# Three weight sums made by adding transfers in HBM, and twelve block pairs in seven products

## The chip, the cores and the metric

The kernel runs on one core of a Trainium2 chip. The metric is device microseconds of that core, the median of three runs. Profiles are of one execution each; times in them count from the start of the execution's span. Engines are named as the profile names them: PE multiplies matrices, DVE and ACT work elementwise, POOL does little here but issue transfers, SP issues nearly all of them.

## The reference

The computation is one decoder layer on 256 tokens plus 16 learned meta tokens, width 2048, all in float32: an RMS norm, one input projection, eight heads of differential attention and four heads of retention side by side, an output projection with a residual add, then a gated MLP and a final RMS norm. Only the MLP matters here:

```python
def conv_glu(u, w_gate, w_up, conv_w, w_down):
    L = u.shape[1]
    g = u @ w_gate
    gp = jnp.pad(g, ((0, 0), (CONV_W - 1, 0), (0, 0)))
    gc = gp[:, 0:L] * conv_w[0]
    for i in range(1, CONV_W):
        gc = gc + gp[:, i:i + L] * conv_w[i]
    return (jax.nn.silu(gc) * (u @ w_up)) @ w_down
...
    u = rmsnorm(h, ffn_norm[l]) * vmask
    h = h + conv_glu(u, w_gate[l], w_up[l], conv_w[l], w_down[l])
```

The hidden width is 5632, 44 blocks of 128. Each weight is used once, so every weight is loaded once.

## The kernel before, in words

Float32 products are made from two halves: a value is rounded to a shorter type (`hi`, by a cast on ACT, L188) and the remainder is kept beside it (`lo`, by a subtraction on DVE, L189). A product is then three matmuls, hi x hi, hi x lo and lo x hi. This is done for the activations and, chunk by chunk as they arrive, for all weights. `load(c)` (L152) issues the load of a chunk of 1 MB on SP's queue, `prep(hf)` splits one half of it (an *entry*), and `ahead(hf)` runs both a few entries before PE needs them: in the down stage loads six entries ahead, splits three.

The stages follow each other: input projection with attention and retention woven in, output projection, then gate and up, then down. **Gate and up** (the loop over `f`, L751) makes one hidden block of 128 per turn: 16 x 3 matmuls for gate, 16 x 2 wider ones for up, then on DVE and ACT the scaling (`g`, L757), the convolution (`c`), the SiLU (`s`), the product `u` and its split into `fhi[:, f]` and `flo[:, f]`. The tiles `g`, `c`, `s` and `ul` (in which `u` stands) have two buffers each.

**Down** multiplies the hidden blocks (256 tokens = two halves m of 128) by `w_down`, four column groups of 512 (n = 2g + j). It runs in two passes g = 0, 1, with two column groups j each. A *plain* entry holds two hidden blocks of one column group, and takes 4 products of 128 x 128 by 128 x 512. The first 20 hidden blocks are handled in 10 *pairs* (`NS = 10`): two hidden blocks, two token halves and two column groups make a 2 x 2 by 2 x 2 block product, which is computed with seven products instead of eight, from sums of activation blocks (*forms*) and sums of weight blocks. The seven products of each pair go to bank (0,0), (0,1), (1,0) and to four extra banks 1, 5, 6, 7, which are joined into the four results at the end of a pass (`joined`, L894).

The forms are made in gate and up when both blocks of a pair are there (L778 to L791): four sums of 128 x 128 on DVE, split into hi and lo, and stored by a POOL transfer to HBM (`sd`). In the down stage SP loads them back (`sf`, L163) ahead of the pair's weights. The weight chunk of a pair (*mixed* chunk) has four blocks of 512 columns, b11, b12, b22, b21. DVE makes four sums from it (L196, L197, L201, L204), each 512 wide, and seven 512-wide operands are split. This is done in four parts, b, d, u, t, each an entry of its own. `down_order()` writes the order of entries out by hand: a few plain entries first, the parts of the pairs with the other plain entries spread evenly between them, a few plain entries last (`LEAD`). Six plain entries of the last column group are held back for the end, where token half 1 is computed in column halves.

SP's queue is in order: a load that waits for its buffer holds the ones behind it. Raw chunks rotate over five buffers in the down stage (three `raw`, `sraw`, and the former `act1`), and `sf` alternates between two (`act2`, `act3`), the room of the activations of earlier stages.

## Time and profile before

| what | value |
|---|---|
| median of three runs | 1166.14 us (1164.39 to 1166.94) |
| profiled execution, its own time | 1161.82 us |
| its span | 1159.9 us |
| PE, DVE, ACT, POOL busy in the span | 1144.7, 919.0, 597.9, 9.7 us |
| moved by the transfers | 240.16 MB, 207 GB/s on average |
| share of SP's queue, of POOL's | 57.7%, 1.3% |

The page gives the busy time of each engine, then 40 slices of 29 us each as digits of tenths, then transfer queues, then the chain of work that ended last, then groups of instructions by line with the names of what they write and read. A group's mean is the duration of one instruction; since neighbours overlap in an engine's pipeline, the distance between starts is shorter. About four per cent of the matmul records are missing in a trace, so their counts are a little low.

### The profile page before, as it was taken

How to read it: one execution, taken by the hardware profiler on the slowest of the kernel's cores; microseconds unless marked ns; L12 is line 12 of the kernel's file. 1: busy time of each engine (PE TensorE's matmuls, PEld its weight loads, DVE VectorE, ACT ScalarE, POOL GpSimd, SP SyncE). 2: the span in 40 equal slices, each digit the busy share in tenths (PEclk: the TensorE clock that was granted, in tenths of full speed). 3: DMA queues.
4: the chain of work that ended last, by engine and by line, in shares of the span. 5: the costliest groups of instructions: out<-in, count | busy, mean ns of one | idle time of the engine just before them, and what ended most of it. 6: DMA issues, size and time to landing. Idle time of an engine off the chain costs nothing.

```text
span 1159.9 us, 20454 instructions
## 1 busy us (share of the span) xinstructions
PE 1144.7 (99%) x7979; PEld 1068.1 (92%) x7979; DVE 919.0 (79%) x1735; ACT 597.9 (52%) x994; POOL 9.7 (1%) x34
## 2 busy tenths in 40 slices
PE   9999999999999999999999999999999999999997
PEld 8999999999999999999999999999999988887876
DVE  7888887667677769777778777777777799999995
ACT  7566665443345445444445444444444455655663
POOL 0000000000000000000000000000000000000000
PEclk9999999999999999999999999999999999999998
DMA  8644546565648777656655555555555477757671
GB/s 308 199 165 159 169 151 185 172 191 165 189 169 246 239 227 262 218 200 220 208 214 210 220 182 183 186 197 194 185 182 181 180 274 273 302 193 285 234 291 72
DMA packets 80991, 240.16 MB, mean 207 GB/s; under 512 B 41858, under 2 KB 49450, under 8 KB 56064
## 3 DMA queue, kind: packets, MB, share of 16 engines
q1 hardware_dynamic: 79024, 232.44, 57.7%
q0 software_dynamic: 1728, 6.29, 1.3%
q8 instruction: 62, 1.02, 0.3%
q14 instruction: 33, 0.27, 0.1%
q10 hardware_dynamic: 144, 0.14, 0.0%
HBM read 227.05 MB, written 11.80 MB: 206 GB/s over the span
## 4 chain that ended last, share of the span: by engine, by line
PE 88%; DVE 5%; DMA 5%; ACT 1%; issue 1%; SPq 0%; DVEq 0%; ACTq 0%
PE mm L443 14%; PE mm L432 10%; PE mm L430 10%; PE mm L431 10%; PE mm L445 7%; PE mm L423 7%; PE mm L422 7%; PE mm L424 7%; PE o L819 4%; PE o L818 4%; PE o L820 4%; DVE wlo L189 1%; DMA rvt<-rhv 1%; DMA raw<-in_w_first_dram 1%; PE x L818 1%; PE x L819 1%
## 5 line engine op out<-in xcount | busy, mean ns | idle before, releaser
L188 ACT CAST whi<-raw 128x1024 fp32r<-128x1024 f32 (+1 forms) x391 | 396.0, 1018 | 385.6 <-PE mm L423 87.0
L189 DVE TENSOR_TENSOR wlo<-raw,whi 128x1024 fp32r<-128x1024 f32 (+1 forms) x391 | 461.5, 1182 | 156.4 <-ACT whi L188 150.5
L443 PE MATMUL mm<-g,whi 128*128 128x512 f32 x704 | 249.1, 392 | 0.0
L422 PE MATMUL mm<-x,whi 128*128 128x272 f32 (+1 forms) x688 | 198.9, 289 | 0.0
L430 PE MATMUL mm<-g,whi 128*128 128x260 f32 x704 | 198.7, 282 | 0.0
L423 PE MATMUL mm<-x,whi 128*128 128x272 f32 (+1 forms) x688 | 198.4, 288 | 0.0
L424 PE MATMUL mm<-x,wlo 128*128 128x272 f32 (+1 forms) x688 | 197.2, 287 | 1.2 <-DVE wlo L189 1.2
L432 PE MATMUL mm<-g,wlo 128*128 128x258 f32 x704 | 198.1, 281 | 0.0
L431 PE MATMUL mm<-g,whi 128*128 128x256 f32 x704 | 194.9, 277 | 0.0
L445 PE MATMUL mm<-g,wlo 128*128 128x256 f32 x660 | 185.1, 281 | 0.0
L443 PEld LDWEIGHTS mm<-g,whi 128*128 128x128 f32 x704 | 132.2, 188 | 25.9
L431 PEld LDWEIGHTS mm<-g,whi 128*128 128x128 f32 x704 | 133.5, 190 | 1.9
L430 PEld LDWEIGHTS mm<-g,whi 128*128 128x128 f32 x704 | 132.2, 188 | 0.0
L432 PEld LDWEIGHTS mm<-g,wlo 128*128 128x128 f32 x704 | 132.0, 187 | 0.0
L424 PEld LDWEIGHTS mm<-x,wlo 128*128 128x128 f32 x688 | 129.6, 188 | 1.4 <-DVE wlo L189 1.4
L422 PEld LDWEIGHTS mm<-x,whi 128*128 128x128 f32 x688 | 129.7, 188 | 0.0
L423 PEld LDWEIGHTS mm<-x,whi 128*128 128x128 f32 x688 | 129.7, 188 | 0.0
L445 PEld LDWEIGHTS mm<-g,wlo 128*128 128x128 f32 x660 | 124.3, 188 | 0.0
L430 PE MATMUL mm<-ys,whi 128*128 128x260 f32 x256 | 71.9, 282 | 0.0
L432 PE MATMUL mm<-ys,wlo 128*128 128x258 f32 x256 | 71.8, 281 | 0.0
L431 PE MATMUL mm<-ys,whi 128*128 128x256 f32 x256 | 70.7, 276 | 0.0
L819 PE MATMUL o<-wlo,fhi 128*128 128x512 f32 x160 | 62.5, 390 | 0.1
(299 smaller groups left out, 1692.7 us busy)
## 6 DMA issues: line engine op xcount, KB each, us to landing
raw<-in_w_in_dram SPq DMA_DIRECT2D x44, 1024.0 KB
raw<-in_w_gate_dram SPq DMA_DIRECT2D x44, 1024.0 KB
raw<-in_w_up_dram SPq DMA_DIRECT2D x44, 1024.0 KB
raw<-in_w_down_dram SPq DMA_DIRECT2D x24, 1024.0 KB
raw<-in_w_mix_dram SPq DMA_DIRECT2D x20, 1024.0 KB
raw<-in_w_out_dram SPq DMA_DIRECT2D x16, 1024.0 KB
sf<-sd SPq DMA_DIRECT2D x20, 512.0 KB
sd<-sh POOLq DMA_DIRECT2D x10, 512.0 KB, 2.9
```

Source lines behind the costliest of these rows:

```text
L188: S.copy(out=hi[:, b:e], in_=src)
L189: V.tensor_tensor(out=lo[:, b:e], in0=src, in1=hi[:, b:e].bitcast(F32), op=ALU.subtract)
L422: PE.matmul(ps[:, :n], wh, xh, start=(k == 0), stop=False)
L423: PE.matmul(ps[:, :n], wh, xl, start=False, stop=False)
L424: PE.matmul(ps[:, :n], wl, xh, start=False, stop=(k == KT - 1))
L430: PE.matmul(ps[:, :NQ + 2], wh, src.cols(k, GO - 2, GL), start=(k == 0), stop=False)
L431: PE.matmul(ps[:, 4:NQ + 2], wh, src.cols(k, GL, GW), start=False, stop=False)
L432: PE.matmul(ps[:, 2:NQ + 2], wl, src.hi(k), start=False, stop=(k == KT - 1))
L443: PE.matmul(ps, wh, src.cols(k, GO + 2, GW), start=(k == 0), stop=(k == KT - 1))
L445: PE.matmul(ps[:, :SEQ], wl, src.cols(k, GO + 2, GL), start=False, stop=False)
L818: PE.matmul(o, ah, wh, start=start, stop=False)
L819: PE.matmul(o, ah, wl, start=False, stop=False)
```

## The change

`NS` goes from 10 to 12: 24 hidden blocks are handled in pairs, and 20 instead of 24 stay plain. The signs of the seven products are arranged differently, so that three of the four weight sums are pure additions of weight blocks. The host's layout puts the blocks in the order w0, w1, w2, w3 (`w_mix`).

The three sums are made in HBM, before the down stage. `sums(g, p0)` takes a batch of two pairs of one pass and lists five POOL transfers, each of which waits for the one before, through their common tile:

1. t23 (two copies) = w3, 1 MB
2. t23 += w0 in both copies, an adding transfer of 1 MB
3. t23[0] += w2, adding, 512 KB
4. t4 = t23[0], 512 KB
5. t4 += w1, adding, 512 KB

Twelve batches make 60 jobs. `paced(t)` puts one job on POOL's queue behind a one-column copy of `t` on POOL; it is called with `g` for each of the 44 blocks and with `u` for every third, 59 times. What is left is issued after the loop.

In the down stage a mixed chunk is loaded by five SP transfers: blocks w0 and w1 (512 KB), the forms (384 KB), t2 and t3 (512 KB), t4 (256 KB), and w2 (256 KB). t4 and w2 go to a tile of their own, `sw`. DVE makes one sum, w2 - w0. The parts are now d, u, c, t: three of 1024 columns and one of 512.

The form S1 (now a difference of two blocks) is stored in `fhi` and `flo` in the place of the block of the pair that no product uses, so three forms instead of four go through HBM. `fhi` and `flo` of that block are filled in their first half only. `act2` and `act3` are each cut in two rooms for `sf` and `sw`. Two joins subtract instead of add.

```diff
-NS = 10
+NS = 12
-PARTS = ("b", "d", "u", "t")
+PARTS = ("d", "u", "c", "t")
+BATCH = 2
+ROOMS = (0, 1, "2a", "2b", "3a", "3b")
...
         if c in mixed:
             g, p = divmod(mixed[c], NS)
-            sf = big.tile([P, 2, 4, P], F32R, tag=f"act{2 + p % 2}", name=f"sf{g}_{p}")
-            keep(nc.sync.dma_start(out=sf.rearrange("p a b c -> p (a b c)").bitcast(F32),
-                                   in_=pools["sd"][p]))
+            sf = big.tile([P, 6 * P], F32R, tag=f"act{2 + p % 2}a", name=f"sf{g}_{p}")
+            sw = big.tile([P, 2 * NW], F32, tag=f"act{2 + p % 2}b", name=f"sw{g}_{p}")
+            td, td4 = pools["td"][g, p]
+            keep(nc.sync.dma_start(out=t[:, :2 * NW], in_=a["w_mix"][g, p][:, :2 * NW]))
+            keep(nc.sync.dma_start(out=sf.bitcast(F32), in_=pools["sd"][p]))
+            keep(nc.sync.dma_start(out=t[:, 2 * NW:], in_=td))
+            keep(nc.sync.dma_start(out=sw[:, :NW], in_=td4))
+            keep(nc.sync.dma_start(out=sw[:, NW:], in_=a["w_mix"][g, p][:, 2 * NW:3 * NW]))
...
-            b11, b12, b22, b21 = [raw[c][:, i * NW:(i + 1) * NW] for i in range(4)]
-            if s == "b":
-                t1 = pools["dn"].tile([P, NW], F32, tag="t1", name=f"t1_{c}")
-                V.tensor_tensor(out=t1, in0=b12, in1=b11, op=ALU.subtract)
-                V.tensor_tensor(out=b12, in0=b22, in1=b12, op=ALU.subtract)
-                raw[c, 1] = t1
-                halves(b11, 0, NW)
-            elif s == "d":
-                V.tensor_tensor(out=b11, in0=b12, in1=b11, op=ALU.add)
-                halves(raw[c][:, 2 * NW:], 0, 2 * NW)
-            elif s == "u":
-                V.tensor_tensor(out=b21, in0=b21, in1=b11, op=ALU.subtract)
-                halves(raw[c][:, :2 * NW], 0, 2 * NW)
+            g, p = divmod(mixed[c], NS)
+            if s == "d":
+                halves(raw[c][:, :2 * NW], 0, 2 * NW)
+            elif s == "u":
+                halves(raw[c][:, 2 * NW:], 0, 2 * NW)
+                V.tensor_tensor(out=raw[c][:, :NW], in0=raw[c][:, 2 * NW:3 * NW],
+                                in1=raw[c][:, :NW], op=ALU.subtract)
+            elif s == "c":
+                halves(pools["sw"][g, p], 0, 2 * NW)
             else:
-                halves(b21, 0, NW)
-                halves(raw.pop((c, 1)), NW, 2 * NW)
+                halves(raw[c][:, :NW], 0, NW)
...
+        def sums(g, p0):
+            n = BATCH
+            t23 = dp.tile([n, P, 2, NW], F32, name=f"t23_{g}_{p0}")
+            t4 = dp.tile([n, P, NW], F32, name=f"t4_{g}_{p0}")
+            t23r = t23.rearrange("n p a c -> (n p) a c")
+            t4r = t4.rearrange("n p c -> (n p) c")
+            w = a["w_mix"][g, p0:p0 + n].rearrange("n p c -> (n p) c")
+            both = lambda i: w[:, i * NW:(i + 1) * NW].unsqueeze(1).to_broadcast([n * P, 2, NW])
+            go = lambda **kw: jobs.append(lambda: keep(nc.gpsimd.dma_start(**kw)))
+            go(out=t23r, in_=both(3))
+            go(out=t23r, in_=both(0), accum_op=ALU.add)
+            go(out=t23r[:, 0], in_=w[:, 2 * NW:3 * NW], accum_op=ALU.add)
+            go(out=t4r, in_=t23r[:, 0])
+            go(out=t4r, in_=w[:, NW:2 * NW], accum_op=ALU.add)
+            for i in range(n):
+                td[g, p0 + i] = (t23[i].rearrange("p a c -> p (a c)"), t4[i])
+
+        def paced(t):
+            if jobs:
+                j = sp.tile([P, 1], F32, tag="pace", name=f"pace{len(jobs)}")
+                keep(nc.gpsimd.tensor_copy(out=j, in_=t[:, 0:1]))
+                jobs.pop(0)()
...
             V.tensor_tensor(out=g, in0=ps[:, :NQ], in1=rstd2, op=ALU.mult)
+            paced(g)
...
-            S.copy(out=fhi[:, f], in_=u)
-            V.tensor_tensor(out=flo[:, f], in0=u, in1=fhi[:, f].bitcast(F32),
+            n = P if f < KP and f % 2 == 0 else SEQ
+            S.copy(out=fhi[:, f, :n], in_=u[:, :n])
+            V.tensor_tensor(out=flo[:, f, :n], in0=u[:, :n], in1=fhi[:, f, :n].bitcast(F32),
                             op=ALU.subtract)
+            if f % 3 == 0:
+                paced(u)
...
+                s1 = fhi[:, f - 1, P:]
+                S.copy(out=s1, in_=sm[:, 0])
+                V.tensor_tensor(out=flo[:, f - 1, P:], in0=sm[:, 0], in1=s1.bitcast(F32),
+                                op=ALU.subtract)
+                sh = fw.tile([P, 2, 3, P], F32R, tag="sh", bufs=1, name=f"sh{p}")
+                S.copy(out=sh[:, 0], in_=sm[:, 1:])
+                V.tensor_tensor(out=sh[:, 1], in0=sm[:, 1:], in1=sh[:, 0].bitcast(F32),
                                 op=ALU.subtract)
...
-                elif y == "b":
-                    product(1, acts(0, 2 * x), wt, 0)
                 elif y == "d":
                     product((0, 0), acts(0, 2 * x + 1), wt, NW)
-                    product((0, 1), forms(x, 3), wt, 0)
+                    product((0, 1), forms(x, 2), wt, 0)
                 elif y == "u":
-                    product(6, forms(x, 1), wt, 0)
-                    product(7, forms(x, 2), wt, NW)
+                    product(6, forms(x, 0), wt, 0)
+                    product(7, forms(x, 1), wt, NW)
+                elif y == "c":
+                    product((1, 0), acts(1, 2 * x + 1), wt, 0)
+                    product(1, acts(0, 2 * x), wt, NW)
                 else:
-                    product((1, 0), acts(1, 2 * x + 1), wt, 0)
-                    product(5, forms(x, 0), wt, NW)
+                    product(5, acts(1, 2 * x), wt, 0)
```

More of the change, by code (lines that the diff above doesn't have):

```diff
@@ L50, with spread, __init__ @@
 LEAD = [(4, 3), (0, HOLD + 3)]
-PARTS = ("b", "d", "u", "t")
+PARTS = ("d", "u", "c", "t")
+BATCH = 2
+ROOMS = (0, 1, "2a", "2b", "3a", "3b")
 RSEQ = [("y", 0), ("g", 0), ("y", 1), ("g", 1), ("y", 2), ("y", 3), ("g", 2), ("g", 3)]
+def spread(tiles):
+    return [(t, i) for t in tiles for i in range(t.shape[1])]
 class Halves:
-    def __init__(self, tiles, off, width, lead=()):
-        self.tiles, self.off, self.width, self.lead = tiles, off, width, lead
-        self.per = KT // len(tiles)
+    def __init__(self, tiles, off, width):
+        self.at, self.off, self.width = spread(tiles), off, width
     def __getitem__(self, ix):
-        k = ix[1]
+        t, i = self.at[ix[1]]
         c = ix[2] if len(ix) > 2 else slice(0, self.width)
-        return self.tiles[k // self.per][(ix[0],) + self.lead + (
-            k % self.per, slice(c.start + self.off, c.stop + self.off))]
+        return t[ix[0], i, c.start + self.off:c.stop + self.off]
 class Packed:
     def __init__(self, tiles):
-        self.tiles = tiles
-        self.per = KT // len(tiles)
+        self.at = spread(tiles)
     def cols(self, k, b, e):
-        return self.tiles[k // self.per][:, k % self.per, b:e]
+        t, i = self.at[k]
+        return t[:, i, b:e]
     def hi(self, k):
@@ L175, in prep @@
         if held < 2:
-            wx = big.tile([P, 2 * 1024], F32R, tag=f"act{2 + held}", name=f"end{held}")
+            hi, lo = [big.tile([P, 1024], F32R, tag=f"act{2 + held}{i}", name=f"end{held}{i}")
+                      for i in "ab"]
         elif c >= nw and (hf - 2 * nw) % 4 == 3:
             wx = big.tile([P, 2 * 1024], F32R, tag="act0", name=f"wx{hf}")
-        else:
-            wx = None
-        if wx is not None:
             hi, lo = wx[:, :1024], wx[:, 1024:]
@@ L706, in trunk_kernel @@
         pump(len(side))
-        gs = Packed([big.tile([P, KT // 4, GW], F32R, tag=f"act{i}", name=f"g{i}")
-                     for i in range(4)])
+        gs = Packed([big.tile([P, KT * n // 8, GW], F32R, tag=f"act{i}", name=f"g{i}")
+                     for i, n in zip(ROOMS, (2, 2, 1, 1, 1, 1))])
         hd = dp.tile([SEQ, D], F32, name="hd")
@@ L795, in trunk_kernel @@
         pools["dn"] = dn
-        pools["sf"], pools["sd"] = {}, sd
+        while jobs:
+            jobs.pop(0)()
+        pools["sf"], pools["sw"], pools["sd"], pools["td"] = {}, {}, sd, td
         fns = {}
@@ L869, in add, with take_off @@
             V.tensor_tensor(out=h, in0=x, in1=h, op=ALU.add)
+        def take_off(h, x):
+            V.tensor_tensor(out=h, in0=h, in1=x, op=ALU.subtract)
         e = 2 * idx
@@ L902, in f2 @@
                     add(t, bank[6])
-                    add(res[0, 1], t)
+                    take_off(res[0, 1], t)
                 def f3():
```

35 lines of the change are left out of this document (20 added, 15 removed).

## The prediction

> **What bounds the kernel now.** I read the page's slices first, then the windows table over the gate and up stage and over stretches of the down stage, then the chain that ended last, then groups and DMA issues.
>
> ```profile
> span 1159.9 us, 20454 instructions
> PE   9999999999999999999999999999999999999997
> DVE  7888887667677769777778777777777799999995
> DMA  8644546565648777656655555555555477757671
> ```
>
> PE is at nine tenths or more in every slice but the last, so only fewer matmuls or fewer stalls can help. In the last seven slices, the down stage, DVE rises to nine tenths and DMA becomes uneven. The profiled execution took 1161.82 us, 1.9 around its span; the median of the three runs, 1166.14, is 4.3 above it. I sum against the span and carry both offsets.
>
> ```profile
> 446.00:920.00 474.00, 474.00 (x3373) 445.29 (x3372) 361.89 (x608) 224.65 (x350) 5.61 (x10) 1.00 0.55 196
> 930.00:940.00 10.00, 10.00 (x45) 8.29 (x45) 9.03 (x13) 6.07 (x8) 0.00 (x0) 1.00 0.97 374
> 1010.00:1020.00 10.00, 10.00 (x46) 8.29 (x45) 9.75 (x13) 6.16 (x9) 0.00 (x0) 1.00 1.00 406
> 1030.00:1040.00 10.00, 10.00 (x46) 8.29 (x45) 10.00 (x15) 6.54 (x13) 0.00 (x0) 1.00 0.05 19
> 1106.00:1108.00 2.00, 2.00 (x11) 1.63 (x10) 1.97 (x3) 0.00 (x0) 0.00 (x0) 1.00 0.90 291
> 1110.00:1120.00 10.00, 9.73 (x43) 7.53 (x41) 9.48 (x13) 6.11 (x9) 0.00 (x0) 1.00 0.99 409
> ```
>
> The columns are PE, PEld, DVE, ACT and POOL busy (instructions), PE clock, DMA share, GB/s. In gate and up PE is busy all 474 us, DVE 362 (76%), POOL 6, and the DMA engines stand at 0.55. In the down stage DVE is close to or at 10 of 10 us; DMA runs at 406 GB/s in one stretch and 19 in another.
>
> ```profile
> L818 PE MATMUL o<-whi,fhi x160: 388/389/504, 920.7 to 1143.5; 128*128 128x512 f32 x160
> ...
> 930.06 0.39 PE L820 MATMUL o<-wx,flo 128*128 128x512 f32 x1
> ...
> 932.33 0.39 PE L818 MATMUL o<-whi,fhi 128*128 128x512 f32 x1
> ...
> 1150.13 0.28 PE L818 MATMUL oe<-end,fhi 128*128 128x256 f32 x1
> ...
> 1151.45 0.28 PE L820 MATMUL oe<-end,flo 128*128 128x256 f32 x1
> ```
>
> Pace: the second and third rows are ten steps of 512-column matmuls in 2.27 us, 0.227 each; the last two are eleven steps of 256 columns in 1.32, 0.12 each. The down stage has 20 pairs' chunks of 7 products and 24 plain chunks of 8, 332 products of three matmuls. Twelve products (the held block of six entries) run as column halves. So 960 x 0.227 + 72 x 0.12 = 226.2 us (0.2267 unrounded), while the stage lasts from 920.7 to 1151.4, 230.7. PE stalls there for only about 4.5 us in all.
>
> ```profile
> 1015.51 0.24 PE o L820
> 1015.82 1.06 ACT whi L188
> ...
> 1024.01 0.60 DVE raw L197
> 1024.61 1.14 DVE wlo L189
> ...
> 1046.95 1.14 ACT whi L188 x2
> 1048.14 0.50 PE o L818
> ...
> 1104.76 7.81 DMA raw<-in_w_mix_dram
> ```
>
> Where those go: from 1015.8 the chain leaves PE and stays on DVE through the sums of L196 to L204, the splits of L189 and the joins, until 1048. The last step shown is a mixed chunk's load that took 7.8 us from SP's issue, just ahead of its use. The chain also gives DVE's back-to-back prices: 0.60 us for a 512-wide operation, 1.14 for a 1024-wide one.
>
> **The change, part by part.**
>
> Products. Two more pairs per group become seven products instead of eight: 4 products over both groups, 12 x 0.2267 = **-2.7 us** of PE. This is on the path, as PE has almost no idle.
>
> DVE sums in the down stage.
>
> ```profile
> L204 DVE TENSOR_TENSOR raw<-raw 128x512 f32<-128x512 f32 x20 | 13.8, 689 | 0.2
> L196 DVE TENSOR_TENSOR t<-raw 128x512 f32<-128x512 f32 x20 | 13.8, 688 | 2.2 <-DMA raw<-in_w_mix_dram 2.1
> ```
>
> These are two of the four sums per mixed chunk, 80 in all. A mixed chunk now costs DVE seven 512-wide operations (four sums, three splits) and two 1024-wide splits: 7 x 0.60 + 2 x 1.14 = 6.5 us. After, one sum, one 512-wide split and three 1024-wide: 4.6. Plain entries cost 1.14. Between two mixed chunks the order puts 17/10 plain entries in group 0 and 15/10 in group 1 before, 13/12 and 11/12 after. PE needs 4.76 us for seven products and 2.72 for a plain entry. So, per mixed chunk with its plain entries, DVE against PE: 8.4 of 9.4 and 8.2 of 8.8 us before, joins and final scaling on top; 5.9 of 7.7 and 5.7 of 7.3 after. In total DVE sheds (20 x 6.48 + 48 x 1.14) - (24 x 4.62 + 40 x 1.14) = 28 us, all off the path except what the 4.5 us of stalls owe to it. Bounds of that term: 0 to -4.5. I take **-3**: the DVE-led stretch before 1048 and the small stalls of group 1 go, some turn-over at the change of groups (take(0,1) and take(1,1) must free banks) stays.
>
> ```profile
> L188 ACT CAST whi<-raw 128x1024 fp32r<-128x1024 f32 x63 | 65.6, 1051 | 39.6 <-DVE raw L201 17.6 <-PE o L820 15.4 <-PE x L820 2.7
> L188 ACT CAST whi<-raw 128x512 fp32r<-128x512 f32 x30 | 18.6, 621 | 19.0 <-DMA raw<-in_w_mix_dram 11.6 <-DVE raw L204 5.8 <-DVE wlo L189 1.2
> ```
>
> ACT's casts go from 20 x (2 x 1.05 + 3 x 0.62) + 48 x 1.05 = 130 to 24 x (3 x 1.05 + 0.62) + 40 x 1.05 = 132 us, a little over half the stage: no term.
>
> Loads in the down stage.
>
> ```profile
> raw<-in_w_down_dram SPq DMA_DIRECT2D x24, 1024.0 KB
> raw<-in_w_mix_dram SPq DMA_DIRECT2D x20, 1024.0 KB
> sf<-sd SPq DMA_DIRECT2D x20, 512.0 KB
> sd<-sh POOLq DMA_DIRECT2D x10, 512.0 KB, 2.9
> ```
>
> Per mixed chunk SP moved 1024 + 512 KB; now 512 + 384 (sf without S1) + 512 + 256 + 256 = 1920 KB, in five issues. With its plain entries that is 2.53 MB per 7.7 us in group 0, 2.45 per 7.25 in group 1: 329 and 337 GB/s, against 263 and 267 before. The window row of 1010 to 1020 shows 406 at share 1.00, so the new demand is 83% of what the engines have done here. I take **0**; cover is the remaining 17% and the five raw buffers.
>
> ```profile
> L164 SPq DMA_DIRECT2D sf<-sd x20: 326/327/424, 919.5 to 1104.3; - x20
> ...
> SPq L164 <- PE x L820: 150.7, 18, 17.6
> ```
>
> SP stood 151 us at the sf load, which could not start until the pair two earlier had used its last form, in the fourth part. After, the forms are used in the first two parts, so sf comes free some 3 us earlier, and half of the raw chunk goes ahead of that wait. Queued behind it are td, t4, the third block and the next plain chunk; td is wanted first, one period and about 1 us after the release, less three entries of preparation (about 4.4 us), and sf and td together take about 2.3 us at 406 GB/s. SP issues three more transfers a chunk at 0.33 us each, inside its waits. The first lands behind four lead entries (10.9 us) as before.
>
> Gate and up: the new work. DVE and ACT make forms for twelve pairs, not ten, with one 128-wide copy and subtract more per pair and one half-width split less; PE, busy for all of the 474 us, covers it, with 24% of DVE free. Without that cover it would be the two pairs' own few microseconds. POOL gets 60 transfers, 59 of them paced by a one-column copy of g (44) or u (15), and each later one of a batch waits on POOL for the one before.
>
> ```profile
> L757 DVE TENSOR_TENSOR fg<-mm,rstd x44: 418/426/429, 446.4 to 917.7; 128x258 f32<-128x258 f32 x44
> ...
> 600.10 0.33 SPq L167 DMA_DIRECT2D raw<-in_w_gate_dram  x1
> ...
> 611.33 0.33 SPq L167 DMA_DIRECT2D raw<-in_w_gate_dram  x1
> ...
> 611.81 1.05 ACT L188 CAST whi<-raw 128x1024 fp32r<-128x1024 f32 x1 [1.46 <-issue]
> ```
>
> g is written from 446.4 to 917.7, one per 11.24 us (issue to issue of the same weight), so five jobs of a batch of two pairs have 471/59 x 5 = 39.9 us. Queued behind POOL's wait are the next copy, the next sd store and, through the two g buffers and the two of u, DVE two blocks later. So POOL may be late by about two blocks, 22.5 us, before DVE, ACT and then PE notice; over 12 batches that makes (471 + 22.5)/12 = 41.1 us a batch.
>
> Price of a batch: no row has an adding transfer or one from HBM to HBM. Nearest is the POOL store, 2.9 us for 512 KB. A batch writes 1.5 MB plainly and 2 MB adding, three and four such units. Low end, adding costs nothing extra: 7 x 2.9 = 20 us. High end, an adding unit costs three passes (read, read, write): 3 x 2.9 + 4 x 8.7 = 43.5. I take two passes, 31.9: the stored 512 KB too were read and written within their 2.9, so reading the destination adds one such pass. That is below 41.1: **0** on the path. The high end costs 12 x (43.5 - 41.1) = +29.
>
> Their effect on weight loads: SP issues one per 5.6 us, and the first cast of the 600.10 load comes at 611.81, so a load of 1 MB may take 11.7 us. Shares: 196 GB/s at 0.55 means 356 at full; a batch at two passes is 5.8 MB, 16 us of all engines in 41, or 0.39, together 0.94. It fits, not by much. The page lists both queues as shares of the same 16 engines:
>
> ```profile
> q1 hardware_dynamic: 79024, 232.44, 57.7%
> q0 software_dynamic: 1728, 6.29, 1.3%
> ```
>
> The Trainium skill, page "DMA: Bandwidth & Descriptors", section "Issuing engines are not separate DMA queues", speaks against treating POOL's queue as its own road: transfers from every issuer run on the same 16 engines and interleave. By it a batch would take 16/0.45 = 36 us instead of my 31.9, an estimate that still ends at 0 but brings the point where the queue falls behind (rival A) down from 2.8 passes to 2.4: 41.1 x 0.45 x 356 GB/s is 6.6 MB, less 1.6 plain, over 2.1 MB. The trace agrees as far as these two rows go.
>
> Sum: 1159.9 - 2.7 - 3 = 1154.2 of span; + 1.9 = 1156.1 for a profiled execution; + 4.3 = **1160.4** for the median.
>
> **Rivals.**
>
> A, slower: POOL's chain of adding transfers is dearer than its slots. Place: POOL, then the g and u buffers, in gate and up. It decides from (41.1 - 8.7)/4 = 8.1 us per adding 512 KB, 2.8 passes; each further us costs 48. At three passes: 1160.4 + 29 = 1189. For it: the engines' 0.94, and the chained waits. Against: 31.9 is 9 below.
>
> B, slower: the loads become the bound of the down stage. Windows like 1106 to 1108 gave 291 GB/s at 0.90. At that rate a period takes 8.7 instead of 7.7 and 8.4 instead of 7.25 us, 12 x (1.0 + 1.16) = 26 us on a floor of 226.2 - 2.7 = 223.5. So 249.5 against 230.7, +18.8: 1185. It decides below 337 GB/s. Against: the 406 and 409, and stretches of 0.05 that leave room.
>
> C, no change: only the products count. The stalls were a change of groups and a late load, not DVE's load, and a microsecond of new waiting for td or for bank (0,1), now wanted by the first part of a pair rather than the second, is added: 1166.1 - 2.7 + 1 = 1164.4.
>
> That the sums don't leave the down stage can't be: POOL's order is the program's, and the last batch is wanted 100 us after gate and up end.
>
> **How the numbers follow.** Forecast 0.55, A 0.20, B 0.10, C 0.15. What a measurement here can tell from no change is about 0.2%, 2.3 us. The forecast lies 5.7 below (its own range 1157 to 1163.5: stalls -4.5 to 0 and 1 us of run scatter); it counts as faster, C as the same, A and B as slower: 0.55, 0.15, 0.30. The range goes from 1157 to 1190, past B and the first half of A; what A may cost beyond three passes is left out.
>
> **What would show it.** Products: 328 of them in the down stage, gate and up still one block per 11.24 us with no PE idle. Sums: L196 to L201 gone and DVE near 8 tenths in the down stage. Down stage: 225 us from first o to last oe. A: POOL copies late after their g, fg writes waiting for POOL, block spacing above 11.24. B: casts that wait for raw, sf or sw with DMA share at 1.0. C: 228 us in the down stage. I am wrong if gate and up get longer at all, or if the down stage stays above 228.

## The result and the profile after

| | before | after |
|---|---|---|
| median | 1165.27 us (1162.58 to 1166.94, 4 runs) | 1215.02 us (1213.61 to 1219.32, 4 runs) |
| ratio | | **1.0435** (1.0402 to 1.0469) |
| profiled execution, span | 1161.82, 1159.9 us | 1219.32, 1217.4 us |

The change made the kernel 50 us slower; the prediction was 1160.4 with a range of 1157 to 1190. The profiled execution of the kernel after is the slowest of its four, so the two profiles lie 57.5 us apart. The page of the changed kernel, its slices, its POOL queue and its chain:

```profile
span 1217.4 us, 20806 instructions
PE   9999999999999999989898999999988959999997
DMA  8554455555567779989998989999988898888881
q0 software_dynamic: 19104, 49.81, 20.2%
PE 50%; DMA 25%; issue 18%; POOL 3%; DVE 3%; ACT 1%; SPq 0%; POOLq 0%; DVEq 0%; ACTq 0%
```

PE has slices of 8 at the 18th, 20th, 22nd, 30th and 31st, which lie in gate and up, and one of 5 at the 33rd, in the down stage. DMA stands at eight and nine tenths from the 16th on, where it mostly stood at five to seven. The chain, 88% PE before, goes through DMA for a quarter of the span. Where the time is, by the tiles `fg` and `fhi` (duration minimum, median, maximum; first and last start) and the last matmul:

```profile
L791 DVE TENSOR_TENSOR fg<-mm,rstd x44: 416/427/429, 447.8 to 955.5; 128x258 f32<-128x258 f32 x44
L862 PE MATMUL o<-whi,fhi x158: 388/394/792, 958.5 to 1201.2; 128*128 128x512 f32 x158
1209.10 0.28 PE L864 MATMUL oe<-end0a,flo 128*128 128x256 f32 x1
```

| stretch | before | after | difference |
|---|---|---|---|
| start to the first g | 446.4 | 447.8 | +1.4 |
| first to last g (gate and up) | 471.3 | 507.7 | +36.4 |
| last g to the first o | 3.0 | 3.0 | 0 |
| first o to the last oe (down) | 230.7 | 250.6 | +19.9 |
| the rest | 8.5 | 8.3 | -0.2 |

So of the 57.5 us nearly two thirds lie in gate and up, where the prediction had 0, and a third in the down stage, where it had a gain of 5.7.

**Gate and up.** Who waits for what from 440 to 960 us (us in total, times, longest), in the changed kernel:

```profile
POOL t L767 <- DMA t<-in_w_mix_dram: 312.2, 28, 15.9
...
ACT sh L829 <- DMA sd<-sh: 45.6, 9, 9.4
...
ACT ful L804 <- POOL pace L783: 21.3, 3, 8.9
```

POOL stands 312 us for transfers out of `w_mix`, plain and adding ones, so its queue is late, and two things stand behind it. One is the pacing copy, which holds a buffer of `g` or `ul`: the last of the three rows. The other is the store `sd`, which reads `sh`, a tile with one buffer: ACT cannot write the next forms until the store has landed. POOL's own sequence around one batch (start, duration, and idle before it):

```profile
721.82 1.22 POOL L767 DMA_DIRECT2D t<-in_w_mix_dram  x1
...
738.47 1.36 POOL L767 DMA_DIRECT2D t<-in_w_mix_dram  x1 [14.31 <-DMA t<-in_w_mix_dram]
739.13 1.28 POOL L832 DMA_DIRECT2D sd<-sh  x1
...
753.18 0.92 POOL L767 DMA_DIRECT2D t<-in_w_mix_dram  x1 [12.54 <-DVE mm L440]
...
763.31 0.59 POOL L767 DMA_DIRECT2D t<-t  x1 [8.83 <-DMA t<-in_w_mix_dram]
...
768.57 0.88 POOL L767 DMA_DIRECT2D t<-in_w_mix_dram  x1 [4.37 <-DVE ful L806]
...
770.07 0.89 POOL L767 DMA_DIRECT2D t<-in_w_mix_dram  x1
```

From one issue to the next: the 1 MB copy 16.7 us, the adding 1 MB 14.7, the adding 512 KB 10.1, the copy of 512 KB 5.3, and the last adding one 1.5, since the next batch has another tile and need not wait. (At 753.18 and 768.57 the profile names DVE as the releaser, which is its inference; each of these jobs also waits for the transfer before it, through their tile.) Over all twelve batches the 60 issues go from 449.6 to 991.2, **45.1 us a batch**; the prediction had 31.9, and 41.1 to spend. The issues and what they took to land (medians; the 1 MB row holds the plain copies and the adding ones, twelve each, and the 512 KB row adding ones alone):

```profile
t<-in_w_mix_dram POOLq DMA_DIRECT2D x24, 1024.0 KB, 14.9
t<-in_w_mix_dram POOLq DMA_DIRECT2D x24, 512.0 KB, 8.5
t<-t POOLq DMA_DIRECT2D x12, 512.0 KB, 5.3
sd<-sh POOLq DMA_DIRECT2D x12, 384.0 KB, 13.8
```

The last row is the one to see: the store of the forms, 2.9 us for 512 KB before, takes 13.8 for 384 KB (2.6 for the same 384 KB in f2 below, which issues no sums). It is issued right behind an adding transfer (738.47 and 739.13 above) and lands about when that one does.

**Down.** The head of the stage has a hole. Its timeline:

```profile
974.34 0.40 PE L864 MATMUL x<-whi,flo 128*128 128x512 f32 x1
974.54 0.90 POOL L767 DMA_DIRECT2D t<-in_w_mix_dram  x1 [8.30 <-DMA t<-in_w_mix_dram]
975.11 0.53 POOL L783 COPY pace<-fg 128x1 f32<-128x1 f32 x1
975.66 0.33 SPq L179 DMA_DIRECT2D raw<-in_w_down_dram  x1
...
987.18 1.22 PE L862 MATMUL o<-whi,fhi 128*128 128x512 f32 x2 [12.45 <-ACT whi L198]
```

What SP's queue waited for between 955 and 1030 us:

```profile
SPq L179 <- POOL pace L783: 12.7, 1, 12.7
```

POOL's last copy of a `g` ran at 975.11. The pool `dn`, in which the raw buffer `sraw` lies, takes the room of `fw`, in which `g` lies; so SP could issue this load only then, and PE stood until 987.18. A second hole of 3.3 us ends at 1006. And steps are longer, here ten of 512 columns in 2.33 us where it was 2.27:

```profile
1025.49 0.39 PE L863 MATMUL o<-wx,fhi 128*128 128x512 f32 x1
...
1027.82 0.39 PE L862 MATMUL o<-whi,fhi 128*128 128x512 f32 x1
```

The 328 products have 948 such steps, and 0.006 us each is 5.7 us. PE is idle for 16.3 us of the stage. Against f2 below, which has this stage without sums in 226.2 us, the 250.6 are 24.4 more: 15 of holes (16.3 against 1.2), 5.7 of longer steps, and 3.6 that the profile does not place, part of them behind the holes, where PE's clock is below full (last section).

### The profile page after: what moved, and what is told of

It reads as the page before. It is cut to its first block, busy times and chain, and to the rows that moved or that the text cites. A ratio compares the mean times of both kernels' runs of the same rounds, so it can differ in the third digit from the quotient of the medians.

```text
span 1217.4 us, 20806 instructions
## 1 busy us (share of the span) xinstructions
PE 1164.3 (96%) x7967; PEld 1078.6 (89%) x7967; DVE 891.0 (73%) x1689; ACT 603.5 (50%) x996; POOL 88.5 (7%) x155
## 3 DMA queue, kind: packets, MB, share of 16 engines
q8 instruction: 62, 1.02, 0.3%
## 4 chain that ended last, share of the span: by engine, by line
PE 50%; DMA 25%; issue 18%; POOL 3%; DVE 3%; ACT 1%; SPq 0%; POOLq 0%; DVEq 0%; ACTq 0%
DMA t<-in_w_mix_dram 14%; PE mm L428 6%; PE mm L429 6%; PE mm L427 6%; PE mm L435 4%; PE mm L437 4%; PE mm L436 4%; PE o L863 3%; PE o L864 3%; PE o L862 3%; DMA sd<-sh 2%; PE mm L448 2%; POOL t L767 2%; PE x L863 1%; PE x L864 1%
## 5 line engine op out<-in xcount | busy, mean ns | idle before, releaser
L199 DVE TENSOR_TENSOR wlo<-raw,whi 128x1024 fp32r<-128x1024 f32 x380 | 455.3, 1200 | 171.7 <-ACT whi L198 168.4
L198 ACT CAST whi<-raw 128x1024 fp32r<-128x1024 f32 x380 | 391.6, 1032 | 367.9 <-PE mm L436 85.5
L448 PE MATMUL mm<-g,whi 128*128 128x512 f32 x352 | 128.1, 401 | 5.2 <-ACT whi L198 5.2
L429 PE MATMUL mm<-x,wlo 128*128 128x272 f32 (+1 forms) x344 | 98.6, 287 | 1.2 <-DVE wlo L199 1.2
L427 PE MATMUL mm<-x,whi 128*128 128x272 f32 (+1 forms) x344 | 99.7, 290 | 0.0
L437 PE MATMUL mm<-g,wlo 128*128 128x258 f32 x352 | 99.4, 282 | 0.0
L435 PE MATMUL mm<-g,whi 128*128 128x260 f32 x352 | 99.2, 282 | 0.0
L428 PE MATMUL mm<-x,whi 128*128 128x272 f32 (+1 forms) x344 | 99.2, 288 | 0.0
L448 PEld LDWEIGHTS mm<-g,whi 128*128 128x128 f32 x352 | 68.0, 193 | 19.2 <-ACT whi L198 5.6
L450 PEld LDWEIGHTS mm<-g,wlo 128*128 128x128 f32 x352 | 68.1, 193 | 2.0 <-DVE wlo L199 2.0
L436 PEld LDWEIGHTS mm<-g,whi 128*128 128x128 f32 x352 | 66.6, 189 | 1.9
L435 PEld LDWEIGHTS mm<-g,whi 128*128 128x128 f32 x352 | 66.1, 188 | 0.0
L437 PEld LDWEIGHTS mm<-g,wlo 128*128 128x128 f32 x352 | 66.0, 188 | 0.0
L427 PEld LDWEIGHTS mm<-x,whi 128*128 128x128 f32 x344 | 64.9, 189 | 0.0
```

Source lines behind the costliest of these rows:

```text
L198: S.copy(out=hi[:, b:e], in_=src)
L199: V.tensor_tensor(out=lo[:, b:e], in0=src, in1=hi[:, b:e].bitcast(F32), op=ALU.subtract)
L427: PE.matmul(ps[:, :n], wh, xh, start=(k == 0), stop=False)
L428: PE.matmul(ps[:, :n], wh, xl, start=False, stop=False)
L429: PE.matmul(ps[:, :n], wl, xh, start=False, stop=(k == KT - 1))
L435: PE.matmul(ps[:, :NQ + 2], wh, src.cols(k, GO - 2, GL), start=(k == 0), stop=False)
```

## The experiments

All ratios are to the kernel before, run on the same chip in between; where there is none, the kernel ran once.

| kernel | us | ratio (interval) |
|---|---|---|
| e1_pad | 1212.75 | 1.0396 (1.0368 to 1.0424) |
| e2_sd_on_sp | 1225.25 | one run |
| e3_own_mark | 1211.11 | one run |
| e4_both | 1182.72 | 1.0174 (1.0136 to 1.0212) |
| f1_shift (of before) | 1167.10 | 1.0038 (1.0025 to 1.0052) |
| f2_no_sums | 1158.11 | 0.9964 (0.9951 to 0.9978) |
| f3_early | 1174.43 | 1.0109 (1.0095 to 1.0123) |
| f4_plain | 1163.36 | one run |
| g1_chain | 1195.59 | 1.0286 (1.0263 to 1.0310) |
| g2_two_sums | 1163.24 | 1.0005 (0.9995 to 1.0015) |
| g3_dve_sums | 1175.62 | 1.0107 (1.0088 to 1.0126) |
| g4_norm_on_pool | 1216.43 | one run |
| h1_norm_first | 1212.08 | 1.0418 (1.0393 to 1.0443) |
| h2_chain_norm | 1194.32 | 1.0275 (1.0242 to 1.0308) |
| i1_scale_late | 1179.09 | 1.0133 (1.0111 to 1.0155) |
| i2_chain_late | 1166.11 | 1.0026 (1.0012 to 1.0041) |
| **j1_mixed** | **1160.15** | **0.9968 (0.9951 to 0.9985)** |

### The longer step

The pacing copy writes a new one-column tile with two buffers of 32 bytes. All that is allocated behind it moves by 64 bytes: in the built programs `fhi` goes from 122368 to 122432. e1 makes those tiles 128 bytes, so that `fhi` stands on a multiple of 256 again; f1 does the reverse, and puts two unused tiles into the kernel before.

```diff
-                j = sp.tile([P, 1], F32, tag="pace", name=f"pace{len(jobs)}")
+                j = sp.tile([P, 32], F32, tag="pace", name=f"pace{len(jobs)}")
...
```

> The changed kernel with the two small pacing tiles widened from 32 to 128 bytes a partition, so that fhi and flo start at a multiple of 256 bytes again (the new pacing tiles had moved them by 64). Theory S (64 bytes): the step from matmul to matmul in the down stage goes back from 0.2327 to 0.2267 us; 984 steps' worth of that, about 5.5 us less in the whole. Rivals (transfers disturb PE's reads of SBUF, or the clock is lower): the step stays at 0.2327 and the time within 2 us of the changed kernel.

```diff
+    gap = [sp.tile([P, 1], F32, tag="gap", name=f"gap{i}") for i in range(2)]
+    for t in gap:
+        V.memset(t, 0.0)
```

> The kernel before with two 32-byte tiles more in front, so that fhi and flo (and ys) start 64 bytes past a multiple of 256. Theory S: the down stage's step goes from 0.2267 to 0.2327 us and the time rises by about 984 x 0.006 = 5.9 us, 0.5%. Rival (the address matters only together with the heavier transfers): no difference.

Ten steps of f1, which is the kernel before but for that place:

```profile
930.20 0.39 PE L823 MATMUL o<-whi,flo 128*128 128x512 f32 x1
...
932.53 0.39 PE L822 MATMUL o<-wx,fhi 128*128 128x512 f32 x1
```

2.33 us, as in the kernel after, and the whole kernel is 0.38% slower, 4.4 us. In e1 the step is back at 0.227. Its ratio is 1.0396 where the kernel after has 1.0435, 4.5 us less, but the intervals overlap; its profiled execution, the slowest of five, had a hole of 16.5 us at the head of the down stage instead of 12.5. The move by 64 bytes is shown as a cause, by f1, of about a tenth of the loss. Which of the moved tiles makes it was not tried apart.

### What stands behind POOL's queue

e2 stores `sd` from SP's queue. e3 lets DVE copy the pacing column to a tile of its own, so POOL no longer holds `g` and `u`. e4 does both, and loads final_norm from SP too.

```diff
-                nc.gpsimd.dma_start(out=sd[p], in_=sh.rearrange("p a b c -> p (a b c)")
+                nc.sync.dma_start(out=sd[p], in_=sh.rearrange("p a b c -> p (a b c)")
```

> The changed kernel with the forms stored by SP's queue instead of POOL's. Theory Q1 (the stalls of gate and up add up, and the first is ACT waiting to rewrite sh while its store stands behind POOL's waits, 45.6 us of waiting): the blocks up to 24 go back to 11.24 us each, 24 us less. Theory Q2 (POOL's chain of 60 transfers, 541 us, sets the end of gate and up through the tiles that its pacing copies hold): the chain still ends near 985 to 990 us, so the early blocks are faster, the later ones slower, and the whole gains under 6 us. Rival R (the weight loads are slowed by the shared engines): no change at all.

```diff
-                keep(nc.gpsimd.tensor_copy(out=j, in_=t[:, 0:1]))
+                q = sp.tile([P, 1], F32, tag="mark", bufs=14, name=f"mark{len(jobs)}")
+                V.tensor_copy(out=q, in_=t[:, 0:1])
+                keep(nc.gpsimd.tensor_copy(out=j, in_=q))
```

> The changed kernel with the pacing copy reading a tile of its own (DVE copies one column of g or u into one of 14 small tiles), so that POOL, when late, holds neither g nor u nor the room of the down stage's first raw buffer. fhi and flo lie at a multiple of 256 bytes. Theory Q: the stall of the forms' store (24 us) stays, the late slowdown (11 us) and the hole of 13.7 us at the head of the down stage go, and with the address 5.5 more: 1215 - 30 = about 1185. Rival R (weight loads slowed by the shared engines): only the address counts, about 1209.

> Forms stored by SP, pacing through tiles of its own, the load of final_norm on SP as well: POOL's queue holds nothing but the sums. All sums are still made. Theory Q: gate and up are back at 11.24 us a block, the down stage starts without a hole and takes about 226 us: 1155 to 1162, at or under the kernel before. Rival R: the transfers' share stays at 0.9 and more and weight loads come late: above 1185.

Waits of e2 over the whole span, and the g writes of e2, e3 and e4:

```profile
ACT ful L804 <- POOL pace L783: 59.5, 8, 11.3
...
DVE fg L791 <- POOL pace L783: 30.0, 9, 6.8
```

```profile
L791 DVE TENSOR_TENSOR fg<-mm,rstd x44: 415/427/429, 451.5 to 959.1; 128x258 f32<-128x258 f32 x44
```

```profile
L793 DVE TENSOR_TENSOR fg<-mm,rstd x44: 417/427/429, 447.7 to 934.0; 128x258 f32<-128x258 f32 x44
```

```profile
L793 DVE TENSOR_TENSOR fg<-mm,rstd x44: 417/426/429, 446.5 to 917.7; 128x258 f32<-128x258 f32 x44
```

Either tie alone still holds the stage. With the store moved, the waits for the pacing copies grow from 21 to 60 us and the stage still takes 508; with the copies freed, the store still costs 15, the stage taking 486. With both moved it takes 471.2, as before, though POOL is as late as ever. e4 in gate and up:

```profile
446.00:920.00 474.00, 474.00 (x3373) 445.41 (x3372) 368.34 (x689) 225.14 (x364) 67.27 (x103) 1.00 0.93 275
```

So the weight loads of this stage do not suffer from 0.93 of the engines in use, and the whole +36.4 came through these two ties.

But the transfers then run on beside the down stage, the last one issued at 1004.5 us in e4, and the times of e3 (expected 1185) and e4 (1155 to 1162) missed. (e2, one run, gained nothing, where its theories had 24 us or up to 6.) In e3 DVE stood 33.1 us for final_norm's load, which POOL issues behind its late transfers; DVE scales it early in the stage (`norm_scale`) and everything behind that on DVE stood too. In e4 SP blocked for 15.7 and 21.4 us instead, as that load waits for room.

g4 puts final_norm's load back on POOL's queue, and is e4 otherwise. h1 and h2 move it ahead of the loop that issues what is left over.

> The kernel with own marks and the sd stores on SP, all five transfers a batch as in the change, but final_norm's load left on POOL's queue. If SP's wait for room for that load caused the holes at the head and at the change of groups in the kernel that had it on SP, these go, but the hole of 32 us at DVE's norm_scale comes back, since POOL's last sums run to about 1005 us: about 1195 to 1205. If the leftover sums themselves disturb the down stage's loads, the time stays at 1180 or above with holes spread over 920 to 1005 and none of 30 us.

```diff
-        while jobs:
-            jobs.pop(0)()
...
         norm(0)
+        while jobs:
+            jobs.pop(0)()
```

> All sums and transfers of the change, own marks, the sd stores on SP; final_norm's load stays on POOL's queue but is issued ahead of the sums that are left over at the end of gate and up, so DVE's norm_scale no longer waits behind them (51.0 us in the kernel that has it behind them). Theory O (the order of POOL's queue made the loss, not the time of the sums themselves): that hole goes whole, 1214.6 - 51 = 1164 of span, some us of late td loads beside the leftover sums: 1160 to 1170 us. Theory R (sums that run on beside the down stage's loads until about 1005 us cost it by themselves): holes at other places take over, as in the kernel with final_norm on SP: 1178 to 1190 us.

g4 and h1, DVE's wait for that load:

```profile
DVE fn L852 <- DMA fn<-in_final_norm_dram: 54.7, 1, 54.7
```

```profile
DVE fn L850 <- DMA fn<-in_final_norm_dram: 46.5, 1, 46.5
```

g4 shows the hole, and at 1216.43 is above its 1195 to 1205. h1 did not remove it, and at 1212.08 is above the ranges of both its theories: 59 of the 60 transfers are issued inside the loop over f, ahead of the load in any case. What was late was POOL, not the program's order. i1 leaves the load where it is and lets DVE use it later:

```diff
-        side.extend([nop] * 12 + [lambda: norm_scale(0)])
...
                     side.extend(joined())
+                    if not g:
+                        side.append(lambda: norm_scale(0))
```

> As the kernel with own marks, sd stores on SP and final_norm on POOL's queue, all five transfers a batch; DVE's norm_scale of group 0 is not put 12 entries into the down stage but behind the joins of group 0, some 110 us into it and just ahead of its first use. Putting the load ahead of the leftover transfers had moved nothing, since nearly all transfers stand in the loop, ahead of it, and POOL is merely late with them. Theory O (what stood behind the late queue made the loss): the hole of 43 to 51 us goes: 1214.6 - 51 = 1164, 1208.1 - 43 = 1165: 1160 to 1170 us. Theory R (sums beside the down stage's loads cost it by themselves): 1178 to 1190, with holes that wait for raw, sf or sw.

1179.09, and the hole is gone; but Theory O had 1160 to 1170, and the time lies in Theory R's 1178 to 1190. i1 in the down stage, over most of the late transfers (the last is issued at 1019.1) and after (columns as in the prediction's windows):

```profile
920.00:1005.00 85.00, 75.29 (x303) 58.26 (x302) 53.97 (x57) 40.21 (x45) 8.56 (x14) 0.94 1.02 335
1005.00:1168.00 163.00, 159.37 (x721) 131.15 (x720) 130.35 (x151) 94.18 (x113) 2.58 (x4) 0.99 0.77 279
```

While the transfers run, the engines are full (1.02), PE is idle for 9.7 of 85 us and its clock is at 0.94. It gets through 303 matmuls, where f2, without sums, has 378 in the same 85 us: 75 steps of 0.227, 17 us, of the 21 by which the stage is longer than in f2. What SP's queue waited for between 920 and 1030 us, two rows of it:

```profile
SPq L179 <- DMA raw<-t: 9.2, 4, 3.0
...
SPq L173 <- DMA t<-in_w_mix_dram: 0.8, 1, 0.8
```

SP stood once for a transfer of the sums, for 0.8 us, and for some 37 us for loads of its own queue to land (0.4 in f2). So the sums were there in time; the loads beside them were slow. Both theories hold a part: the ties, with the moved tiles, cost some 35 us (1.0435 to 1.0133), and sums that run beside the down stage's loads cost the rest, 15 against the kernel before and some 20 against f2.

### The sums themselves

f2 issues no sums: the down stage loads blocks of `w_mix` of the same sizes instead, and the three sums are left out. f4 keeps all transfers but makes the adding ones plain, so the additions are left out.

```diff
-            for p in range(0, NS, BATCH):
-                sums(g, p)
+            for p in range(NS):
+                m = a["w_mix"][g, p]
+                td[g, p] = (m[:, 2 * NW:], m[:, NW:2 * NW])
...
```

> The changed kernel without the 60 POOL transfers: the down stage loads unsummed blocks of w_mix in their place, in the same sizes (the three sums are left out, all else is computed). fhi and flo lie at a multiple of 256 bytes. It prices the down stage's part of the change alone. Theory Q with the prediction's sum: gate and up at 11.24 us a block, down stage 224 to 226 us, 1159 to 1162. Rival B of the prediction (83% of the engines' rate is too near): casts wait for loads, down stage 232 or more, 1168 and up.

```diff
-            go(out=t23r, in_=both(0), accum_op=ALU.add)
+            go(out=t23r, in_=both(0))
...
```

> The changed kernel with the three adding transfers of each batch made plain ones of the same bytes (the additions are left out, so the sums are wrong; all else is as in the changed kernel). If adding is what costs (a second read and the addition), a batch falls from 45 us to 35 or less, POOL keeps up, and the time is near 1165. If any HBM to HBM transfer in 2 KB rows beside the loads is that slow, a batch stays at 42 or more and the time above 1195.

f2's windows, and what f4's transfers took to land:

```profile
446.00:920.00 474.00, 474.00 (x3373) 445.34 (x3372) 362.86 (x630) 225.33 (x364) 6.73 (x12) 1.00 0.55 197
921.00:1147.00 226.00, 224.78 (x1020) 185.86 (x1018) 183.11 (x205) 134.41 (x158) 1.10 (x2) 1.00 0.80 294
```

```profile
t<-in_w_mix_dram POOLq DMA_DIRECT2D x24, 1024.0 KB, 9.9
t<-in_w_mix_dram POOLq DMA_DIRECT2D x24, 512.0 KB, 5.9
t<-t POOLq DMA_DIRECT2D x12, 512.0 KB, 5.6
```

f2 is what the down stage can be with the same loads: 226.2 us from first o to last oe against 230.7, PE idle for 1.2 of 226, the whole 0.36% faster. f4 keeps pace with the blocks (g from 448.8 to 920.1). An addition makes 512 KB take 8.5 instead of 5.9 us, and 1 MB 15.0 instead of 9.9 (15.0 is the average from the issue of the adding 1 MB to the next, in the kernel after), about one and a half times; and a plain 512 KB from HBM to HBM already takes twice the 2.9 of the store that I priced it by.

f2 lies just under its 1159 to 1162, f4 with 1163.36 near its 1165.

f3 spreads the jobs over the output projection as well, 16 there and 44 by g, with e4's marks and SP's stores.

```diff
+            paced(hT)
             if j == 0:
                 S.activation(out=acc2, in_=hT, func=AF.Square)
...
-            if f % 3 == 0:
-                paced(u)
```

> All sums made, but their transfers start in the output projection (one behind each of its 16 columns, one behind each of the 44 blocks), pacing through tiles of its own, forms stored by SP; final_norm's load stays with POOL. Theory Q: the chain of some 541 us ends near 880, before the down stage; no stall in gate and up, no hole, 1158 to 1163: under the kernel before. If shared engines matter in the down stage only while sums run beside it (from 920 to 1005 in the run with both repairs), this is gone too. Rival R: above 1175.

At 1174.43 it missed its 1158 to 1163. Its windows from 400 us to the first g and over the down stage, and two waits:

```profile
400.00:464.00 64.00, 56.15 (x416) 54.10 (x415) 38.96 (x81) 25.12 (x42) 8.51 (x12) 0.95 1.01 277
...
938.00:1164.00 226.00, 225.09 (x1021) 186.20 (x1020) 183.41 (x206) 134.57 (x158) 1.53 (x3) 1.00 0.81 298
```

```profile
ACT whi L198 <- DMA raw<-in_w_out_dram: 19.4, 6, 5.9
DVE hb L764 <- DMA hd<-hb: 18.3, 5, 5.1
```

The down stage is as good as in f2, 225.9 us: the last sum is issued at 937.5, just ahead of it. But the output projection's stores (`hb` to `hd`, pieces of 32 columns) and weight loads stood for the sums, and it ended 17.8 us late. The window of the kernel before, 400 to 446, has the engines at 0.81 already.

g3 has no sums in HBM and makes all four on DVE, so it is the change without its transfers.

```diff
+            w0, w1, w2, w3 = [raw[c][:, i * NW:(i + 1) * NW] for i in range(4)]
+            t2 = pools["sw"][g, p][:, :NW]
             if s == "d":
                 halves(raw[c][:, :2 * NW], 0, 2 * NW)
+                V.tensor_tensor(out=w3, in0=w3, in1=w0, op=ALU.add)
...
```

> The twelve pairs in seven products and S1 in its new place stay, but no sum is made in HBM: DVE makes all four in the down stage, and a mixed chunk is one load of 1 MB again, with sf behind it. So this is the change without its transfers. DVE then has four sums, five 512-wide splits and one 1024-wide split for a mixed chunk: 9 x 0.60 + 1.14 = 6.5 us, with its plain entries 7.8 of 7.7 us in group 0 and 7.6 of 7.3 in group 1. Theory V (DVE's relief is worth something only because DVE is at its limit, so without it DVE becomes the bound): the down stage is 24 x 6.54 + 40 x 1.14 = 203 us of DVE for splits and sums with joins and squares on top, 232 to 240 us against 230.7 before: 1163 to 1172 us, no gain. Theory C (the relief is worth nothing, only the products count): 227 to 229 us of down stage, 1159 to 1162.

```profile
924.00:1168.00 244.00, 234.96 (x1020) 186.39 (x1019) 226.32 (x329) 139.03 (x206) 1.10 (x2) 0.99 0.59 221
```

DVE is busy for 226 of 244 us and the stage is 13 us longer than before: Theory V, and a little more. So the twelve pairs pay only if DVE is rid of most of the sums.

### Fewer sums in HBM

g1 makes each batch of six transfers of 512 KB (t3 = w3, t3 += w0, t2 = t3, t2 += w2, t4 = t2, t4 += w1), adding 1.5 MB instead of 2; for the 72 jobs `u` paces two blocks of three. h2 is g1 with h1's edit, i2 with i1's. g2 makes t2 and t3 only; DVE makes t4.

```diff
-            go(out=t23r, in_=both(3))
-            go(out=t23r, in_=both(0), accum_op=ALU.add)
-            go(out=t23r[:, 0], in_=w[:, 2 * NW:3 * NW], accum_op=ALU.add)
+            go(out=t23r[:, 1], in_=w[:, 3 * NW:])
+            go(out=t23r[:, 1], in_=w[:, :NW], accum_op=ALU.add)
+            go(out=t23r[:, 0], in_=t23r[:, 1])
+            go(out=t23r[:, 0], in_=w[:, 2 * NW:3 * NW], accum_op=ALU.add)
...
```

> All three sums of the change stay in HBM, but each batch is six transfers of 512 KB instead of five with two of 1 MB: t3 = w3, t3 += w0, t2 = t3, t2 += w2, t4 = t2, t4 += w1. So 1.5 MB a batch is added instead of 2 and 1.5 MB copied as before. The pacing copies read their own marks, the sd stores go on SP's queue, fhi stands where it stood before. Theory P (the price of the adding transfers set the end; in the changed kernel an adding 512 KB took about 8 us and a plain 512 KB about 5): 3 x 8 + 3 x 5 = 39 us a batch, 468 in all against 475 us of gate and up, so POOL's queue just keeps up or trails by less than the 22 us of slack; gate and up keep 11.24 us a block, the down stage is 226 to 229: 1157 to 1163 us. Theory Q (it was the number of bytes beside the weight loads, whatever their kind, or the number of waits, that made POOL late): six waits a batch instead of five, so POOL ends later than in the kernel with both edits, beyond 1005 us, and the down stage is disturbed again: 1180 or more.

> The same order of POOL's queue with six transfers of 512 KB a batch, whose chain ended at about 980 us. Theory O: 1198.4 - 38.5 = 1160 of span, 0 to 3 us less as the leftover sums end 25 us sooner than in the kernel with five: 1157 to 1163 us. Theory R: 1170 us or more.

> The same late norm_scale with six transfers of 512 KB a batch. Theory O: 1198.4 - 38.5 = 1160, 1188.4 - 29.3 = 1159: 1156 to 1163 us. Theory R: 1170 or more.

> Only t3 = w3 + w0 and t2 = t3 + w2 are made in HBM, four transfers of 512 KB a batch; t4 = t2 + w1 is made by DVE in the down stage (0.6 us for each of 24 chunks, 14 us over the stage), and its load goes. Marks, sd stores on SP and the place of fhi as in the six-transfer kernel. Theory P: 2 x 8 + 2 x 5 = 26 us a batch, 312 in all, so the queue is done at about 770 to 930 by its pacing and nothing waits for it; gate and up 446 to 918; DVE in the down stage still has 5.9 + 0.6 of 7.7 us: 226 to 228 us of down stage, 1156 to 1160 us. Theory Q: any sum made beside the loads costs some us in gate and up or at the head of the down stage: 1163 or more.

g1 missed: its jobs ran from 450.6 to 977.5, 44 us a batch and not 39, because an adding 512 KB landed in 9 us and a plain one in 6.6; DVE stood 40.3 us for final_norm, in h2 30.7. With that wait gone i2 is at 1.0026, 3 us above the top of what Theory O gave. Its late transfers still run 65 us into the stage, the last issued at 985.9, and PE gets through 268 matmuls there against 289 in f2, 5 us behind; the whole stage takes 234.7. g2's last transfer is issued at 834 us and disturbs nothing; but with DVE's 24 sums the down stage takes 229.1 us, so most of f2's gain is gone. There is no difference to the kernel before, and the expected 1156 to 1160 is missed.

j1 puts the two together: three sums in HBM for group 0, two for group 1, whose t4 DVE makes.

```diff
+                if g:
+                    V.tensor_tensor(out=pools["sw"][g, p][:, :NW], in0=raw[c][:, 2 * NW:3 * NW],
+                                    in1=raw[c][:, NW:2 * NW], op=ALU.add)
...
```

> The sums are cut to what fits into gate and up: all three in HBM for group 0 (six transfers of 512 KB a batch, 44 us a batch in the kernel that made them all so), two for group 1 (four transfers, 29 us), whose t4 = t2 + w1 DVE makes in the down stage. Own marks, sd stores on SP, norm_scale where the change has it. Theory O+R (queue order and the overrun of the sums into the down stage are the whole loss): 6 x 44 + 6 x 29 = 438 us from 449, so the queue ends at about 890, before the down stage and before final_norm's load; gate and up 11.24 us a block; down stage 226.2 us as without any sums plus at most 1.5 us for DVE's twelve sums: 1157 to 1161 us, faster than the kernel before by 0.1 to 0.5%. Rival D (DVE's sums, not the overrun, make the 229 us of the kernel with two sums, and the adding transfers still cost some us): 1162 to 1165, no difference.

Its transfers, and the windows of gate and up and of the down stage:

```profile
L768 POOL DMA_DIRECT2D t<-in_w_mix_dram x42: 581/883/1777, 450.8 to 880.3; - x42
```

```profile
446.00:920.00 474.00, 474.00 (x3373) 445.29 (x3373) 368.43 (x692) 224.68 (x365) 66.71 (x120) 1.00 0.88 264
923.00:1150.00 227.00, 225.06 (x1021) 185.77 (x1019) 190.05 (x220) 134.67 (x158) 1.12 (x2) 1.00 0.76 281
```

The last transfer is issued at 880, PE loses nothing in gate and up and 2 us in the down stage, and the kernel is 0.32% faster than the one before: it beats i2 and g2, and comes as far below the kernel before as f2 without any sums (0.36%).

## Why the prediction was wrong

**The step that failed** is the price of a batch, "I take two passes, 31.9". It measured 45.1, above the 41.1 that the slots and buffers allowed. Of the two factors in it, one held roughly: an adding transfer costs about 1.5 times a plain one, where I took twice. The other did not: the base, 2.9 us for 512 KB, came from a store out of on-chip memory. Plain 512 KB between two places in HBM, beside the same weight loads, took 5.3 to 5.9. By POOL's issue times the five jobs of a batch took 14.6, 15.0, 8.7, 5.9 and 1.0 us on average. The first is a plain copy, but it runs beside the last addition of the batch before; in the first batch, with no addition beside it, it took 8.7. So some 14.6 us (8.7 and 5.9) belong to the plain 1.5 MB, which I priced at 8.7, and the other 30.6 to the adding 2 MB, priced at 23.2. Neither excess alone uses up the 9.2 that were left; together they do. Which difference from the store makes the base dearer (HBM at both ends, shorter rows, the sums' own traffic) was not tried apart. My high end, 43.5, was below the measurement as well. The estimate by the Trainium skill, page "DMA: Bandwidth & Descriptors", section "Issuing engines are not separate DMA queues", was 36 us: nearer, and right in direction. That transfers of different issuers share the same engines fits i1, where SP's loads come late beside POOL's sums at a share of 1.02.

**Rival A** came true in its result and partly in its place (POOL's chain, then the buffers of g and u, but the store of the forms too). Its threshold of 8.1 us per adding 512 KB was not what decided: the four such units of a batch took (15.0 + 2 x 8.5)/4 = 8.0, and it had left the plain ones at 8.7 in all. Its own formula at 45.1, 12 x 4.0 = 48 us more, gives 1208, which is near 1215 partly by luck: gate and up lost 36.4, and A had nothing for the down stage. I had cut the range off at three passes. Its chance of 0.20 rested on "31.9 is 9 below", that is on the wrong base.

**The slack** of 22.5 us left out a tie that I had named. I wrote that the next sd store stands behind POOL's wait, and followed only the g and u buffers from there. `sh` has one buffer, written again two blocks later, and out of the same 22.5 us come POOL's delay ahead of the store and the store itself, which went from 2.9 to 13.8. What a late POOL did at the head of the down stage, through the room of `fw`, was not in the sum at all. And I had set aside sums that run on into the down stage, because the last batch is wanted 100 us later; they cost there all the same, through final_norm's load behind them and through the loads beside them.

**Not foreseen**: the 5.7 us of the moved tiles (4.4 in f1).

**Right**: with no sums issued the products and DVE's relief come to 4.5 us of the stage (230.7 to 226.2) where I had 5.7, and to 0.36% of the time; PE's floor of 223.5 leaves 2.7 us of stalls where I had 1.5. The loads of the down stage alone cost nothing that shows (f2, 0.80 of the engines), so B was wrong for them; its sign, casts that wait for loads at a share of 1.0, appears where sums run beside them (i1). C was wrong too, as f2's stage is below its 228. The block rhythm of 11.24 us held in e4, i1 and j1. The engines' share of 0.94 that I worked out for gate and up was 0.93 in e4, partly by luck: a batch took 46.3 us there and not the 41 of the estimate, so it kept the engines for some 17.6 us (0.38 of 46.3) and not 16. That much traffic was harmless to loads of 1 MB with 11.7 us to land. My forecast of 1160.4 and j1's 1160.15, with fewer transfers, agree by chance: beside j1 the kernel before took 1163.50, so its gain is 3.4 us where I had 5.7.

**Open**: why the loads of the down stage are slow beside the sums while those of gate and up are not. The share of the engines is 1.02 against 0.93, but the runs do not separate the share from the loads' own sizes and order.

## What to carry to other kernels

Price a transfer by a row of its own kind (from where, to where, beside what), and where there is none, take the dear end and ask what happens then: a queue that falls behind is only as harmless as everything that stands behind it. List those, down to the buffer count of each: stores, copies that hold a buffer, loads used by an engine that works in order, and rooms that a later stage takes over. Work moved off an engine should end before the next stage needs the road that it uses, and it may pay to move less of it.

## What the runs showed of the hardware

- Moving the tiles behind the small ones by 64 bytes, the stationary operands `fhi` and `flo` among them, lengthened a step of 512 columns in the down stage from 0.227 to 0.233 us (f1, the kernel 0.38% slower). Why, and by which tile, was not tried.
- A small store issued behind an adding transfer on the same queue took about as long as that transfer: 384 KB in 13.8 us, against 6.0 behind the plain ones of f4 and 2.6 in f2, where nothing stands ahead of it.
- PE's granted clock was lower in a hole and behind it. Windows of the kernel after, in the hole and behind it:

```profile
975.00:990.00 15.00, 2.78 (x6) 1.77 (x7) 2.45 (x2) 2.09 (x2) 1.23 (x3) 0.62 0.89 277
990.00:1005.00 15.00, 12.68 (x51) 9.87 (x49) 7.67 (x9) 8.29 (x9) 1.46 (x2) 0.93 1.05 377
```

So a stall costs a little more than its length: 0.93 over the 15 us behind it is about 1 us.
